# Squares of the residual taken early, the norm products placed later, rope tables inside the FFN, and the scores of two heads issued in turn into two banks

## The chip, the cores and the metric

The kernel runs on one core of one Trainium2 chip. The metric is the device time of one execution in microseconds, as the median of three runs. All times in this document are microseconds (us) unless marked ns. The engines are named as in the profile: PE is TensorE (PEld its weight loads), DVE is VectorE, ACT is ScalarE, POOL is GpSimd, SP is SyncE, which issues the DMAs.

## What is computed

Two networks of two layers each work one after the other on a residual stream x of 512 tokens by 1024 channels, in fp32 throughout. Each layer is a mixer followed by a gated FFN, and each of these eight parts has a norm before and a norm after:

```python
for l in range(2):                       # first block
    h = rms_norm(x, mix_norm_pre[l]) * (1.0 + sc_m) + sh_m
    y = hybrid_mixer(h, ...)             # 8-head attention over 256 selected keys, and a 4-head mLSTM
    x = x + g_m * rms_norm(y, mix_norm_post[l])
    h = rms_norm(x, ffn_norm_pre[l]) * (1.0 + sc_f) + sh_f
    y = swiglu(h, w_gate_up[l], w_down[l])
    x = x + g_f * rms_norm(y, ffn_norm_post[l])
# second block: the same frame, with another attention mixer, a convolution in the FFN, no modulation
```

The selection in the first block's attention takes, for each block of 128 queries, `relu(q_idx . k_idx)` of 8 index heads, weighted and summed, and keeps the top keys as a mask; the attention scores of each of the 8 heads (64 channels each) are then taken densely and masked.

## The kernel before, in words

All activations are kept transposed: 8 tiles (index k, `KT` = 8) of 128 channels by 512 tokens. Every large product is three fp32r products (`mm3`): high part of the weight with high part of the activation (`whi`, `hh`), `whi` with the low part `hl`, and `wlo` with `hh`. `load` (L261 to 267) brings a weight chunk by DMA into `raw`, copies it to `whi` on ACT and takes `wlo = raw - whi` on DVE.

**The passage from one part to the next.** The last projection of a part is computed in two halves of 256 tokens (`in_halves`): all output chunks for the first half, then the chunks in reverse order for the second half, the last few with weights that were kept. While PE computes the second half of the old projection, the first half goes through `post_norm` and `pre_norm`; while PE computes the first half of the next projection (`fm_split`), the second half goes through them. `post_norm` sums the squares of y with a product against a matrix of ones (tiles `nrm<-ssy`, `nrm<-sql`), takes the reciprocal root on ACT (`rstd`) and then on DVE does 8 times y * g * rstd (`yn`, L488) and x + yn (L489). `pre_norm` then squares the eight tiles of x on ACT (`sq<-x`, L444), adds them in pairs on DVE (L446), sums the four results over the channels with four products against ones (`nrm<-sq`), takes `rstd`, and writes `xn` (DVE L458), `hh` (ACT L462) and `hl` (DVE L473).

Where these products stand in PE's stream is set by numbers: `LA` = 2 and `LB` = 1 are the chunk of the old projection's second half before which the first half's `pre_norm` is called (after a mixer and after an FFN), `LC` = 4 and `LD` = 2 the chunk of the next projection's first half before which the second half's `pre_norm` (`pending`) is called. A scheduler then fixes one order per engine at build time; each engine runs its own list strictly in that order, waiting on semaphores. There are seven passages with a `pre_norm`: four from a mixer to its FFN (called M here), three from an FFN to the next mixer (called F).

**Rope tables.** At the start of the FFN of the first block's second layer, `rope_tables` computes cos and sin of the second block's positions: 128 x 512 operations on DVE and two Sin on ACT. In the FFNs `tick` advances a generator (`self.back`) by two steps after every chunk.

**Mixer of the first block.** Work is cut into generators whose steps a planner (`timeline`) merges by due times from a table (`T1`). `index(t)` makes the index scores of query block t (t = 1, 2, 3; 8 heads, (t + 1) * 128 keys); `topk(t)` turns them into a mask on DVE; `attend(hd)` makes for one head and t = 0 to 3 the scores (one plain fp32 product of 64 rows), adds mask and takes the row maximum on DVE (L872), and exponentiates on ACT; `attout(hd)` transposes the weights on PE and multiplies them with the values. Scores go into the two PSUM banks of the pool `pj`, which the projections of the same mixer use too. The two heads of a pair lie in rows 0 to 63 and 64 to 127 of the same tiles.

Of the kernel before, what the change touches and what calls it, by code (L numbers as in the profile page):

```python
# [10 lines left out]
F32 = mybir.dt.float32  # L11
# [3 lines left out]
ALU = mybir.AluOpType  # L15
# [23 lines left out]
PD1 = 0  # L39
PD2 = 0  # L40
EARLY = 6
PAIRS = 4
PH1 = 0
PH2 = 0
PXM = 0
SA = 0
LA = 2
LAG = 3
LOA = 40
NO = 7  # L50
LB = 1
LC = 4
LD = 2
WIN = 0
KF = 3
KM = 1
# [130 lines left out]
class Net:  # L187
# [174 lines left out]
    def norms(self, y, sqs, g, nxt, late):  # L362


        if nxt is None:
            steps = [lambda i=i: self.post_norm(HALVES[i], y, sqs, g, True) for i in range(2)]
            return {0: steps[0]}, steps[1], (None, None)
        h = self.new_h()
        post = [lambda i=i: self.post_norm(HALVES[i], y, sqs, g) for i in range(2)]
        pre = [lambda i=i: self.pre_norm(HALVES[i], *nxt, *h) for i in range(2)]  # L370
        self.pending = pre[1]
        if late == 0:
            return {0: lambda: (post[0](), pre[0]())}, post[1], h
        return {0: post[0], late: pre[0]}, post[1], h

    def fm_split(self, chunks, act, pool, more=None):

        tiles = [self.ps("pj" if i < PJ else "ps") for i, _ in enumerate(chunks)]  # L380

        begin = {LC if more is None else LD: self.pending}
        middle = {} if more is None else {0: lambda: run(steps(more, 4))}
        self.in_halves([(i, [src]) for i, src in enumerate(chunks)], KF if more is None else KM,
                       lambda i, ws, hs, _: self.fm(tiles[i], ws[0], 0, act, hs, range(KT)), pool,
                       begin, middle)
        return tiles
# [46 lines left out]
        run(self.tok_steps(*args))  # L434


    def pre_norm(self, hs, gs, sh, hh, hl):

        nc, x = self.nc, self.x
        ps = self.ps("nrm")  # L440
        sq = None
        for k in range(KT):
            s2 = self.half("sq")
            nc.scalar.activation(s2, x[k][:, hs], AF.Square)  # L444
            if sq is not None:
                nc.vector.tensor_tensor(s2, sq, s2, ALU.add)  # L446

            sq = s2 if k < 2 * PAIRS and k % 2 == 0 else None
            if sq is None:
                self.matmul(ps[:, :256], self.ones, s2, start=k == min(1, PAIRS), stop=k == KT - 1)  # L450
        r = self.half("rstd")
        self.ln_exp_rstd(ps[:, :256], r, D)
        ts = []
        for k in range(KT + LAG):
            if k < KT:
                t = self.half("xn")
                ts.append(t)
                nc.vector.scalar_tensor_tensor(t, x[k][:, hs], gs[:, k:k + 1], r, ALU.mult, ALU.mult)  # L458
                if sh is None:
                    nc.scalar.activation(hh[k][:, hs], t, AF.Copy)  # L460
                else:
                    nc.scalar.activation(hh[k][:, hs], t, AF.Identity, bias=sh[:, k:k + 1])  # L462
            if k >= LAG:
                j = k - LAG
                lo, hi = hl[j][:, hs], hh[j][:, hs].bitcast(F32)
                pool = (PH2 if sh is None else PH1) >> j & 1
                if sh is None:
                    (nc.gpsimd if pool else nc.vector).tensor_tensor(lo, ts[j], hi, ALU.subtract)
                elif pool:
                    nc.scalar.activation(ts[j], ts[j], AF.Identity, bias=sh[:, j:j + 1])  # L470
                    nc.gpsimd.tensor_tensor(lo, ts[j], hi, ALU.subtract)
                else:
                    nc.vector.scalar_tensor_tensor(lo, ts[j], sh[:, j:j + 1], hi, ALU.add, ALU.subtract)  # L473
# [68 lines left out]


    def rope_tables(self, pos):
        nc = self.nc
        cos = self.cp.tile([P, T], F32, tag="cos", name=self.nm("cos"))
        sin = self.cp.tile([P, T], F32, tag="sin", name=self.nm("sin"))
# [5 lines left out]
        for tab, turn in ((sin, 0.0), (cos, 0.25)):  # L553
            n = self.unit("n")
            nc.vector.tensor_scalar(n, ang, 1.0 / TWO_PI, turn, ALU.mult, ALU.add)
            nc.vector.tensor_scalar(n, n, MAGIC, None, ALU.add)
            nc.vector.tensor_scalar(n, n, MAGIC, None, ALU.subtract)
            r = self.unit("r")
            nc.vector.scalar_tensor_tensor(r, n, -C1, ang, ALU.mult, ALU.add)
            nc.vector.scalar_tensor_tensor(r, n, -C2, r, ALU.mult, ALU.add)  # L560
            nc.vector.scalar_tensor_tensor(r, n, -C3, r, ALU.mult, ALU.add)
            if turn:
                nc.vector.tensor_scalar(r, r, math.pi / 2, None, ALU.add)
            nc.vector.tensor_scalar(r, r, PI_IN, -PI_IN, ALU.min, ALU.max)
            self.act(tab, r, AF.Sin)
        self.cos, self.sin = cos, sin

    def rope(self, pa, pb, n=P):
# [39 lines left out]
    def scores(self, ps, q, k, n, qs):  # L608

        mm = self.matmul  # L610
        mm(ps[:, :n], q[:, qs], k[0][:, :n], start=True, stop=False)
        mm(ps[:, :n], q[:, qs], k[1][:, :n], start=False, stop=True)

    def softmax(self, ps, n, mask, gate=None):

# [63 lines left out]
    def mix1(self, l, h, nxt, feed=None):  # L679
# [126 lines left out]
        def index(t):  # L806
# [1 line left out]
            qs = slice(t * P, n)  # L808
            a = masks[t] = self.unit("ia")
            for hh in range(8):  # L810
                ps = self.ps("is")
                r = slice(64 * (hh % 2), 64 * (hh % 2) + 64)
                self.matmul(ps[:, :n], qi[hh // 2][r, qs], ki[r, :n], start=True, stop=True)
                w = cols[:, t, 4 + hh:5 + hh]
                if hh == 0:
                    nc.vector.tensor_scalar(a[:, :n], ps[:, :n], 0.0, w, ALU.max, ALU.mult)
# [43 lines left out]
            ka[g] = pairs(*self.rope(pa, pb))  # L860
            yield

        def attend(hd):
            g, i = divmod(hd, 4)
            r = slice(64 * (i % 2), 64 * (i % 2) + 64)
            probs[hd] = []
            for t in range(NB):
                n = (t + 1) * P
                ps, p = self.ps("pj"), self.unit("p")
                st = self.sp.tile([P, 1], F32, tag="st1", bufs=8, name=self.nm("st"))  # L870
                self.matmul(ps[:, :n], qa[g][i // 2][r, t * P:n], ka[g][i // 2][r, :n], start=True, stop=True)
                nc.vector.tensor_tensor_reduce(p[:, :n], ps[:, :n], self.tri if t == 0 else masks[t][:, :n], -0.125, 3.4e38,  # L872
                                               ALU.add, ALU.min, st)
                yield
                self.act(p[:, :n], p[:, :n], AF.Exp, bias=st, scale=-1.0)
                probs[hd].append(p)
                yield

        def attout(hd):
# [33 lines left out]
        s0, s1, ahead = w("at")  # L913
        d = (s1 - s0) / (8 + ahead)
        sc, at = [], []
        for hd in range(8):
            sc.append(Task(attend(hd), 8, s0 + d * hd, s0 + d * (hd + 1), {0: [pj[hd // 4]], 2: [tk[0]], 4: [tk[1]], 6: [tk[2]]}))
            at.append(Task(attout(hd), 13, s0 + d * (hd + ahead), s0 + d * (hd + ahead + 1), {0: [sc[hd], va_] + at[-1:]}))
        more = [Task(self.modulation(0, (2, 3, 4)), 24, *w("md"))] if l == 0 else []
        timeline(up_, va_, *cv, *ix, *tk, *pj, *ml, *sc, *at, *more)  # L920

# [174 lines left out]
    def block1(self, upto=None):  # L1096
# [20 lines left out]
        for l in range(2):  # L1117
# [11 lines left out]
                return t  # L1129

            if l == 1:
                self.rope_tables(A["positions_2"])
            gu, dn = A["w1_gu"][l], A["w1_dn"][l]
            h = self.ffn(h, lambda f, i: gu[2 * f + i], evict, lambda f, p: self.down_chunks(dn, f, p), self.modc(l, 5), nxt, (PF1, PD1))
            if upto == (1, l, "ffn"):
# [599 lines left out]
```

## Time and profile before

| | |
|---|---|
| median of 3 runs (lowest, highest) | 3197.48 us (3195.80, 3197.76) |
| profiled execution: own time, span | 3197.12 us, 3195.4 us |
| PE busy | 3044.9 us (95%) |
| PEld busy | 2545.4 us (80%) |
| DVE busy | 2013.8 us (63%) |
| ACT busy | 1548.1 us (48%) |
| POOL busy | 67.1 us (2%) |
| mean granted clock of TensorE | 0.978 |
| HBM read, written | 336.19 MB, 8.42 MB |

The span runs from the first to the last instruction of the profiled execution; the 1.7 us between it and that execution's own time lie around the instructions. Busy time of PE counts overlapping products once and includes the time that a product takes to drain, so that a busy PE is not one at its peak. Idle time of an engine counts for the end only where nothing else is on the way to it, so a wait is to be judged in its own stretch of the program. A granted clock of 1.00 is TensorE's upper level (2.4 GHz), 0.50 its lower (1.2 GHz).

### The profile page before, as it was taken

What the parts mean: (1) busy time and instruction counts of PE and PEld (TensorE: products, weight loads), DVE (VectorE), ACT (ScalarE), POOL (GpSimd) and SP (SyncE); (2) the same over time, 40 slices, a digit from 0 to 9 for tenths busy, and PEclk for the clock granted to TensorE, in tenths of its full rate; (3) what the DMA queues carried; (4) which work ended last, traced back from release to release, by engine and by line L of the source; (5) the groups of instructions that cost most, each with busy time, mean ns of one, the idle gap of its engine ahead of it and who ended that gap; (6) DMA issues with size and microseconds to landing.
All of it is one profiled execution on the core that took longest, in us unless ns stands there. A gap on an engine that the chain in (4) does not pass through costs nothing.

```text
span 3195.4 us, 42599 instructions
## 1 busy us (share of the span) xinstructions
PE 3044.9 (95%) x16196; PEld 2545.4 (80%) x16196; DVE 2013.8 (63%) x3692; ACT 1548.1 (48%) x2760; POOL 67.1 (2%) x179
## 2 busy tenths in 40 slices
PE   8998899998999899999999999999989999999998
PEld 6764788888875788888988779888888877898887
DVE  7887575546786563236676677635577766776365
ACT  4435542234445642234477665434445866454343
POOL 0000000000000000000000100000000001000000
PEclk9998999999999999999999999999999999999999
DMA  7244266644331232324421124333243112332323
GB/s 240 88 158 154 95 220 195 208 133 147 110 99 59 93 109 81 114 84 136 132 67 40 60 73 146 103 99 102 89 158 109 40 47 73 112 126 79 113 87 108
DMA packets 118925, 358.40 MB, mean 112 GB/s; under 512 B 15408, under 2 KB 28464, under 8 KB 118720
## 3 DMA queue, kind: packets, MB, share of 16 engines
q1 hardware_dynamic: 118720, 355.68, 34.2%
q8 instruction: 127, 2.08, 0.3%
q14 instruction: 78, 0.64, 0.1%
HBM read 336.19 MB, written 8.42 MB: 108 GB/s over the span
## 4 chain that ended last, share of the span: by engine, by line
PE 70%; issue 13%; DVE 10%; ACT 3%; DMA 3%; POOL 1%; SPq 0%; POOLq 0%; DVEq 0%; ACTq 0%
PE ps L305 28%; PE op L305 12%; PE pj L305 11%; PE dn L305 7%; PE tk L305 3%; PE po L305 2%; PE nrm L305 2%; DMA wm<-in_w_mod_dram 2%; DVE wlo L267 2%; DVE yn L488 1%; PE pt L308 1%; DVE x L489 1%; DVE wm L633 1%; DVE ss L1479 1%; PE cmp L305 1%
## 5 line engine op out<-in xcount | busy, mean ns | idle before, releaser
L267 DVE TENSOR_TENSOR wlo<-raw,whi 128x1024 fp32r<-128x1024 f32 (+1 forms) x562 | 628.7, 1123 | 577.8 <-ACT whi L265 575.4
L265 ACT ACTIVATE whi<-raw 128x1024 fp32r<-128x1024 f32 (+1 forms) x562 | 550.2, 980 | 803.3 <-PE ps L305 199.4
L305 PE MATMUL ps<-hh,whi 128*128 128x512 f32 (+1 forms) x1560 | 574.2, 368 | 0.0
L305 PE MATMUL ps<-hh,wlo 128*128 128x512 f32 (+1 forms) x1560 | 573.2, 367 | 0.0
L305 PE MATMUL ps<-hl,whi 128*128 128x512 f32 (+1 forms) x1560 | 572.5, 367 | 0.0
L305 PE MATMUL pj<-hh,whi 128*128 128x512 f32 (+1 forms) x944 | 352.8, 375 | 14.6 <-ACT hh L654 8.3
L305 PE MATMUL pj<-hl,whi 128*128 128x512 f32 (+1 forms) x944 | 351.5, 372 | 0.7 <-DVE hl L655 0.7
L305 PE MATMUL pj<-hh,wlo 128*128 128x512 f32 (+1 forms) x944 | 350.7, 371 | 0.1
L305 PEld LDWEIGHTS ps<-hh,wlo 128*128 128x128 f32 x1560 | 295.3, 189 | 48.8 <-DVE wlo L267 0.6
L305 PEld LDWEIGHTS ps<-hh,whi 128*128 128x128 f32 x1560 | 295.6, 189 | 48.1
L305 PEld LDWEIGHTS ps<-hl,whi 128*128 128x128 f32 x1560 | 295.3, 189 | 47.9
L305 PEld LDWEIGHTS pj<-hh,whi 128*128 128x128 f32 x944 | 179.5, 191 | 54.1 <-ACT hh L654 10.6
L305 PEld LDWEIGHTS pj<-hh,wlo 128*128 128x128 f32 x944 | 179.7, 190 | 30.3 <-issue 1.2
L305 PEld LDWEIGHTS pj<-hl,whi 128*128 128x128 f32 x944 | 179.8, 190 | 29.6 <-DVE hl L655 1.7
L633 DVE CUSTOM_DVE_ANT_0 wm<-wm,cact 128x1024 f32<-128x1024 f32 x96 | 116.9, 1221 | 108.4 <-DMA wm<-in_w_mod_dram 108.2
L305 PE MATMUL op<-hidh,whi 128*128 128x256 f32 (+1 forms) x572 | 178.5, 312 | 0.0
L305 PE MATMUL op<-hidh,wlo 128*128 128x256 f32 (+1 forms) x572 | 177.1, 310 | 0.3 <-DVE wlo L267 0.3
L305 PE MATMUL op<-hidl,whi 128*128 128x256 f32 (+1 forms) x572 | 176.5, 309 | 0.0
L305 PE MATMUL dn<-hidl,whi 128*128 128x512 f32 x352 | 137.0, 389 | 0.1
L305 PE MATMUL dn<-hidh,wlo 128*128 128x512 f32 x352 | 136.9, 389 | 0.0
L305 PE MATMUL dn<-hidh,whi 128*128 128x512 f32 x352 | 136.9, 389 | 0.0
L275 ACT ACTIVATE p<-p,st 128x128 f32<-128x128 f32 (+3 forms) x192 | 106.2, 556 | 57.7 <-DVE st L872 38.7
(350 smaller groups left out, 5804.0 us busy)
## 6 DMA issues: line engine op xcount, KB each, us to landing
raw<-in_w_in_dram SPq DMA_DIRECT2D x134, 512.0 KB, 3.4
raw<-in_w_up_dram SPq DMA_DIRECT2D x100, 512.0 KB, 3.5
wm<-in_w_mod_dram SPq DMA_DIRECT2D x96, 512.0 KB, 4.6
raw<-in_w_gu_dram SPq DMA_DIRECT2D x94, 512.0 KB, 3.5
raw<-in_w_dn_dram SPq DMA_DIRECT2D x80, 512.0 KB, 3.5
raw<-in_w_out_dram SPq DMA_DIRECT2D x52, 512.0 KB, 3.6
raw<-in_w_dn_dram SPq DMA_DIRECT2D x80, 192.0 KB, 3.1
hp<-rp SPq DMA_DIRECT2D x96, 64.0 KB, 2.0
```

The costliest lines, as they stand in the source:

```text
L265: nc_.scalar.activation(hi[:, :n], raw[:, :n], AF.Copy)
L267: (self.lo_eng or nc_.vector).tensor_tensor(lo[:, :n], raw[:, :n], hi[:, :n].bitcast(F32), ALU.subtract)
L275: j = self.nc.scalar.activation(out, in_, func, **kw).ins
L305: return self.paced(self.nc.tensor.matmul(*args, **kw))
L308: return self.paced(self.nc.tensor.transpose(*args))
L488: nc.vector.scalar_tensor_tensor(t, y(k, hs), g[:, k:k + 1], r, ALU.mult, ALU.mult)
L489: (nc.gpsimd if PXM >> k & 1 else nc.vector).tensor_tensor(self.x[k][:, hs], self.x[k][:, hs], t, ALU.add)
L633: self.nc.vector.tensor_tensor_reduce(raw, raw, self.cact, 1.0, 0.0, ALU.mult, ALU.add, self.mod[l][:, c:c + 1])
L1479: nc.vector.tensor_tensor_scan(s[:, c][:, ::-1], a[:, c][:, ::-1], a[:, c][:, ::-1], 0.0, ALU.add, ALU.bypass)
```

## The change

Four things, all in the order in which the same arithmetic is issued:

1. **Squares early, products late.** `pre_norm` loses its squares. A new `squares` (ACT squares, DVE pair sums) is called straight behind `post_norm` of the same half, and `pre_norm` begins with the four products. The first half's products are called two chunks later (`LA` 2 to 4, `LB` 1 to 3), the second half's one chunk later into an FFN (`LC` 4 to 5). Into a mixer they move from the first half of the projection (`LD`, dropped) to between the halves (`between`): one token step first where there are 3 chunks, none where there are 4, then the products, then the rest of four token steps. `PAIRS` (always pairs now) and the case `late == 0` go.
2. **Rope tables in steps.** `rope_steps` yields six times; the second layer's FFN takes it as its `self.back`, two steps per chunk.
3. **Index scores** of two heads are issued one behind the other (`two`), the second tied behind the first, into two banks, before the first is read.
4. **Attention scores**: `attend` takes a pair of heads instead of one; both products first, then both DVE operations, one step later both exponentials. Four tasks of 8 steps stand where there were eight of 8, over the same due times.

```diff
-LA = 2
+LA = 4
-LB = 1
-LC = 4
-LD = 2
+LB = 3
+LC = 5
...
         h = self.new_h()
-        post = [lambda i=i: self.post_norm(HALVES[i], y, sqs, g) for i in range(2)]
-        pre = [lambda i=i: self.pre_norm(HALVES[i], *nxt, *h) for i in range(2)]
-        self.pending = pre[1]
-        if late == 0:
-            return {0: lambda: (post[0](), pre[0]())}, post[1], h
-        return {0: post[0], late: pre[0]}, post[1], h
+        sq = {}
+
+        def post(i):
+            self.post_norm(HALVES[i], y, sqs, g)
+            sq[i] = self.squares(HALVES[i])
+
+        pre = lambda i: self.pre_norm(HALVES[i], sq[i], *nxt, *h)
+        self.pending = lambda: pre(1)
+        return {0: lambda: post(0), late: lambda: pre(0)}, lambda: post(1), h
...
-        begin = {LC if more is None else LD: self.pending}
-        middle = {} if more is None else {0: lambda: run(steps(more, 4))}
+        def between():
+            early = 4 - len(chunks)
+            run(steps(more, early))
+            self.pending()
+            run(steps(more, 4 - early))
+
+        begin, middle = ({LC: self.pending}, {}) if more is None else ({}, {0: between})
...
+    def squares(self, hs):
+
+        nc, x, res = self.nc, self.x, []
         for k in range(KT):
             s2 = self.half("sq")
             nc.scalar.activation(s2, x[k][:, hs], AF.Square)
-            if sq is not None:
-                nc.vector.tensor_tensor(s2, sq, s2, ALU.add)
-
-            sq = s2 if k < 2 * PAIRS and k % 2 == 0 else None
-            if sq is None:
-                self.matmul(ps[:, :256], self.ones, s2, start=k == min(1, PAIRS), stop=k == KT - 1)
+            if k % 2:
+                nc.vector.tensor_tensor(s2, res[-1], s2, ALU.add)
+                res.pop()
+            res.append(s2)
+        return res
+
+    def pre_norm(self, hs, sqs, gs, sh, hh, hl):
+
+        nc, x = self.nc, self.x
+        ps = self.ps("nrm")
+        for i, sq in enumerate(sqs):
+            self.matmul(ps[:, :256], self.ones, sq, start=i == 0, stop=i == len(sqs) - 1)
...
+    def two(self, tag, q, k, n, qs):
+
+
+        pss, last = [self.ps(tag) for _ in range(2)], None
+        for i, ps in enumerate(pss):
+            r = slice(64 * i, 64 * i + 64)
+            j = self.matmul(ps[:, :n], q[r, qs], k[r, :n], start=True, stop=True).ins
+            if last:
+                self.behind(j, last)
+            last = j.name
+        return pss
...
-                ps = self.ps("is")
-                r = slice(64 * (hh % 2), 64 * (hh % 2) + 64)
-                self.matmul(ps[:, :n], qi[hh // 2][r, qs], ki[r, :n], start=True, stop=True)
+                if hh % 2 == 0:
+                    pair = self.two("is", qi[hh // 2], ki, n, qs)
+                ps = pair[hh % 2]
...
-                ps, p = self.ps("pj"), self.unit("p")
-                st = self.sp.tile([P, 1], F32, tag="st1", bufs=8, name=self.nm("st"))
-                self.matmul(ps[:, :n], qa[g][i // 2][r, t * P:n], ka[g][i // 2][r, :n], start=True, stop=True)
-                nc.vector.tensor_tensor_reduce(p[:, :n], ps[:, :n], self.tri if t == 0 else masks[t][:, :n], -0.125, 3.4e38,
-                                               ALU.add, ALU.min, st)
-                yield
-                self.act(p[:, :n], p[:, :n], AF.Exp, bias=st, scale=-1.0)
-                probs[hd].append(p)
+                pss = self.two("pj", qa[g][i], ka[g][i], n, slice(t * P, n))
+                mask = self.tri if t == 0 else masks[t][:, :n]
+                ps_st = []
+                for ps in pss:
+                    p = self.unit("p")
+                    st = self.sp.tile([P, 1], F32, tag="st1", bufs=8, name=self.nm("st"))
+                    nc.vector.tensor_tensor_reduce(p[:, :n], ps[:, :n], mask, -0.125, 3.4e38, ALU.add, ALU.min, st)
+                    ps_st.append((p, st))
+                yield
+                for j, (p, st) in enumerate(ps_st):
+                    self.act(p[:, :n], p[:, :n], AF.Exp, bias=st, scale=-1.0)
+                    probs[2 * pr + j].append(p)
                 yield
...
             if l == 1:
-                self.rope_tables(A["positions_2"])
+                self.back = self.rope_steps(A["positions_2"])
```

How the change moves instructions is shown at three places.

**PE, first passage F** (first block, first layer, second half of the FFN's down projection: `op` are its chunks, 33 products each). Before, the four products on the squares stand 28 products behind the last product of the post norm (`nrm<-sql`):

```order
L305 MATMUL op_6539<-hidl_6090,whi_6468 128x256
L305 MATMUL op_6539<-hidh_6089,wlo_6469 128x256
L305 MATMUL nrm_6577<-sq_6580,ones 128x256
L305 MATMUL nrm_6577<-sq_6586,ones 128x256
L305 MATMUL nrm_6577<-sq_6592,ones 128x256
L305 MATMUL nrm_6577<-sq_6598,ones 128x256
L305 MATMUL op_6649<-hidh_5346,whi_6638 128x256
```

Now the first two stand 63 products behind it, two products into the third chunk (`op_6630`), and the other two 31 products further on:

```order
L303 MATMUL op_6580<-hidh_6060,wlo_6576 128x256
L303 MATMUL op_6630<-hidh_5317,whi_6619 128x256
L303 MATMUL op_6630<-hidl_5318,whi_6619 128x256
L303 MATMUL nrm_6668<-sq_6512,ones 128x256
L303 MATMUL nrm_6668<-sq_6517,ones 128x256
L303 MATMUL op_6630<-hidh_5317,wlo_6620 128x256
```

In the second half of F the first of these products stood 40 products behind `nrm<-sql` and stands 57 behind it now. In M, first half, 45 became 93; in M, second half, 24 products on the first half of the tokens lie behind them before the first product that reads the second half, where 48 lay before.

**ACT, the same passage.** Before, the eight squares stand behind the square of the next chunk's y (`sqy`), which waits for DVE:

```order
L275 ACTIVATE rstd_6512<-rstd_6512 128x256
L265 ACTIVATE whi_6688<-raw_6687 128x1024
L265 ACTIVATE whi_6694<-raw_6693 128x384
L1084 ACTIVATE sqy_6574<-y_3792 128x256
L444 ACTIVATE sq_6578<-x_3159 128x256
L444 ACTIVATE sq_6580<-x_3160 128x256
```

Now they stand ahead of it, and of two more weight splits:

```order
L263 ACTIVATE whi_6625<-raw_6624 128x384
L448 ACTIVATE sq_6510<-x_3130 128x256
L448 ACTIVATE sq_6512<-x_3131 128x256
L448 ACTIVATE sq_6515<-x_3132 128x256
L448 ACTIVATE sq_6517<-x_3133 128x256
L448 ACTIVATE sq_6520<-x_3134 128x256
L448 ACTIVATE sq_6522<-x_3135 128x256
L448 ACTIVATE sq_6525<-x_3136 128x256
L448 ACTIVATE sq_6527<-x_3137 128x256
L263 ACTIVATE whi_6709<-raw_6708 128x1024
L263 ACTIVATE whi_6715<-raw_6714 128x384
L1117 ACTIVATE sqy_6565<-y_3783 128x256
```

The square of y follows behind, and on DVE the first two pair sums now stand directly behind the sixteen operations of the post norm, with a weight split (`wlo`) between the second and the third sum.

**PE, attention scores** (first block, first layer; `pj<-hp,hp` are scores, both operands' tiles hold two heads). Before, neighbours are mostly of one head:

```order
L305 MATMUL pj_2254<-hp_1826,hp_1687 128x384
L305 MATMUL pj_2275<-hp_1827,hp_1688 128x128
L305 MATMUL pj_2293<-hp_1827,hp_1688 128x256
L305 MATMUL num_1994<-w_2247,vm_151 128x128
L305 MATMUL pj_2316<-hp_1827,hp_1688 128x384
L305 MATMUL pj_2353<-hp_1826,hp_1687 128x512
```

Now the two heads of a pair follow each other, but the scheduler has put another product between some:

```order
L303 MATMUL pj_2236<-hp_1833,hp_1696 128x384
L303 MATMUL pj_2237<-hp_1833,hp_1696 128x384
L303 MATMUL pj_2276<-hp_1834,hp_1697 128x128
L303 MATMUL pj_2277<-hp_1834,hp_1697 128x128
L303 MATMUL pj_2318<-hp_1834,hp_1697 128x256
L303 MATMUL num_2001<-w_2256,vm_151 128x128
L303 MATMUL pj_2319<-hp_1834,hp_1697 128x256
```

Of the 32 pairs of scores 22 are neighbours now, and 10 have one product between them; of the 24 pairs of index scores all are neighbours, where 20 were before.

## Rows read from the trace of the kernel before

**Rows 1.** The page, part 1: busy us, share of the span, instructions.
```profile
PE 3044.9 (95%) x16196; PEld 2545.4 (80%) x16196; DVE 2013.8 (63%) x3692; ACT 1548.1 (48%) x2760; POOL 67.1 (2%) x179
```
**Rows 2.** PE's waits by releaser: us in total, times, longest us.
```profile
PE nrm L305 <- DVE sq L446: 48.3, 11, 7.1
PE pj L305 <- DVE st L872: 11.8, 7, 7.7
```
**Rows 3.** Timeline, PE, four passages: start, us, what, [idle before, releaser].
```profile
375.45 0.80 PE L305 MATMUL nrm<-sq,ones 128*128 128x256 f32 x1 [3.74 <-DVE sq L446]
...
752.39 3.78 PE L305 MATMUL nrm<-sq,ones 128*128 128x256 f32 x8 [5.78 <-DVE sq L446]
...
782.75 1.13 PE L305 MATMUL nrm<-sq,ones 128*128 128x256 f32 x4 [2.54 <-DVE sq L446]
...
1141.81 3.86 PE L305 MATMUL nrm<-sq,ones 128*128 128x256 f32 x8 [7.13 <-DVE sq L446]
```
**Rows 4.** Windows, PE, five half-clock stretches at M: us, PE busy (x), PEclk, DMA.
```profile
374.60:381.40 6.80, 5.95 (x20) 0.50 0.45 155
...
sum 27.30, PE 21.92; mean PE 4.38
```
**Rows 5.** Windows, PE, the five half-clock stretches at F.
```profile
sum 30.80, PE 23.73; mean PE 4.75
```
**Rows 6.** Timeline, PE, behind the wait at 752 us: steps at both clocks.
```profile
756.40 0.41 PE L305 MATMUL op<-hidh,wlo 128*128 128x256 f32 x1
756.61 0.41 PE L305 MATMUL op<-hidh,whi 128*128 128x256 f32 x1
...
757.33 0.28 PE L305 MATMUL op<-hidh,wlo 128*128 128x256 f32 x1
757.45 0.28 PE L305 MATMUL op<-hidh,whi 128*128 128x256 f32 x1
```
**Rows 7.** Timeline, PE, the last product of the post norm there.
```profile
742.57 0.70 PE L305 MATMUL nrm<-sql,ones 128*128 128x256 f32 x2
```
**Rows 8.** Timeline, DVE, the same passage: post norm, split, pair sums.
```profile
744.26 0.88 DVE L488 SCALAR_TENSOR_TENSOR yn<-y,mod,rstd 128x256 f32<-128x256 f32 x2 [2.20 <-ACT rstd L275]
...
749.45 0.75 DVE L489 TENSOR_TENSOR x<-x,yn 128x256 f32<-128x256 f32 x2
...
750.45 1.22 DVE L267 TENSOR_TENSOR wlo<-raw,whi 128x1024 fp32r<-128x1024 f32 x1
...
751.92 0.75 DVE L446 TENSOR_TENSOR sq<-sq,sq 128x256 f32<-128x256 f32 x2
```
**Rows 9.** Timeline, ACT, the same passage: squares, rstd, first hh.
```profile
750.88 2.54 ACT L444 ACTIVATE sq<-x 128x256 f32<-128x256 f32 x8
756.21 0.48 ACT L275 ACTIVATE rstd<-nrm,eps 128x256 f32<-128x256 f32 x1 [2.78 <-PE nrm L305]
...
757.69 0.51 ACT L462 ACTIVATE hh<-xn,mod 128x256 fp32r<-128x256 f32 x1 [0.55 <-DVE xn L458]
```
**Rows 10.** Timeline, DVE, ahead of the wait at 1141 us: the rope tables begin.
```profile
1133.49 0.42 DVE L551 CAST ang<-pi 128x512 f32<-128x512 int32 x1
```
**Rows 11.** Windows, all engines: a passage F; the mixers of layers 0 and 1.
```profile
743.00:776.00 33.00, 26.23 (x189) 24.97 (x188) 26.48 (x55) 18.46 (x37) 0.00 (x0) 0.90 0.39 123
260.00:270.00 10.00, 1.92 (x6) 0.92 (x7) 10.00 (x23) 2.84 (x5) 0.00 (x0) 0.77 0.43 144
990.00:1050.00 60.00, 57.84 (x207) 30.48 (x206) 31.51 (x94) 42.30 (x86) 1.46 (x5) 0.95 0.14 44
```
**Rows 12.** Timeline, PE, index scores, one product (two records) and what follows.
```profile
135.12 1.12 PE L305 MATMUL is<-ki,hp 64*128 64x512 f32 x2
136.17 0.39 PE L305 MATMUL tk<-whi,hh 128*128 128x256 f32 x1
```
**Rows 13.** Timeline, PE, index scores of two heads (four records) and what follows.
```profile
139.24 1.13 PE L305 MATMUL is<-ki,hp 64*128 64x512 f32 x4
140.30 0.50 PE L305 MATMUL pj<-hh,whi 128*128 128x512 f32 x1
```
**Rows 14.** Timeline, DVE, the operation on a score of 512 keys.
```profile
268.95 0.67 DVE L872 CUSTOM_DVE_ANT_0 p<-pj,ia 128x512 f32<-128x512 f32 x1
```

More of the change, by code (lines that the diff above doesn't have):

```diff
@@ L41 @@
 EARLY = 6
-PAIRS = 4
 PH1 = 0
@@ L434, in tok @@
         run(self.tok_steps(*args))
[L437 to L441, printed above, removed]
+    def squares(self, hs):
+        nc, x, res = self.nc, self.x, []
         for k in range(KT):
@@ L544, in rope_tables, with rope_steps @@
     def rope_tables(self, pos):
+        run(self.rope_steps(pos))
+    def rope_steps(self, pos):
         nc = self.nc
@@ L561, in rope_tables @@
             nc.vector.scalar_tensor_tensor(r, n, -C3, r, ALU.mult, ALU.add)
+            yield
             if turn:
@@ L565, in rope_tables @@
             self.act(tab, r, AF.Sin)
+            yield
         self.cos, self.sin = cos, sin
@@ L861, in attproj, with attend @@
             yield
[L863 to L866, printed above, removed]
+        def attend(pr):
+            g, i = divmod(pr, 2)
+            probs[2 * pr], probs[2 * pr + 1] = [], []
             for t in range(NB):
                 n = (t + 1) * P
-                ps, p = self.ps("pj"), self.unit("p")
-                st = self.sp.tile([P, 1], F32, tag="st1", bufs=8, name=self.nm("st"))
-                self.matmul(ps[:, :n], qa[g][i // 2][r, t * P:n], ka[g][i // 2][r, :n], start=True, stop=True)
-                nc.vector.tensor_tensor_reduce(p[:, :n], ps[:, :n], self.tri if t == 0 else masks[t][:, :n], -0.125, 3.4e38,
-                                               ALU.add, ALU.min, st)
+                pss = self.two("pj", qa[g][i], ka[g][i], n, slice(t * P, n))
[6 more added lines that the diff above has]
+                    ps_st.append((p, st))
                 yield
-                self.act(p[:, :n], p[:, :n], AF.Exp, bias=st, scale=-1.0)
-                probs[hd].append(p)
+                for j, (p, st) in enumerate(ps_st):
+                    self.act(p[:, :n], p[:, :n], AF.Exp, bias=st, scale=-1.0)
+                    probs[2 * pr + j].append(p)
                 yield
@@ L915, in mix1 @@
         sc, at = [], []
+        for pr in range(4):
+            sc.append(Task(attend(pr), 8, s0 + d * 2 * pr, s0 + d * 2 * (pr + 1), {0: [pj[pr // 2]], 2: [tk[0]], 4: [tk[1]], 6: [tk[2]]}))
         for hd in range(8):
-            sc.append(Task(attend(hd), 8, s0 + d * hd, s0 + d * (hd + 1), {0: [pj[hd // 4]], 2: [tk[0]], 4: [tk[1]], 6: [tk[2]]}))
-            at.append(Task(attout(hd), 13, s0 + d * (hd + ahead), s0 + d * (hd + ahead + 1), {0: [sc[hd], va_] + at[-1:]}))
+            at.append(Task(attout(hd), 13, s0 + d * (hd + ahead), s0 + d * (hd + ahead + 1), {0: [sc[hd // 2], va_] + at[-1:]}))
         more = [Task(self.modulation(0, (2, 3, 4)), 24, *w("md"))] if l == 0 else []
```

## The prediction

> **What bounds the kernel now.** I read the page's busy line first, then PE's waits grouped by releaser, the timeline of PE at those waits, PE's granted clock behind them, and last DVE and ACT in the same stretches. PE is busy 3044.9 us of 3195.4, 95% [rows 1], and its list is strictly in order, so any time that PE loses is the kernel's. Little is idle, and it sits in few places. PE waits 11 times for a pair sum of squares, 48.3 us together [rows 2]: 3.74 us in the first half of each of the four passages M, 5.78 us in the first half of each of the three F, 2.54 us in the second half of the first F, and 7.13 us in one second half of M [rows 3]; 48.3 - 4 x 3.74 - 3 x 5.78 - 2.54 - 7.13 = 6.3 us are left for the second halves of the other two F.
>
> Each wait costs twice. Behind them stand ten stretches at a granted clock of 0.50, the lower level of 1.2 GHz; PE is busy in them 21.92 us at M and 23.73 us at F [rows 4, 5]. There a product follows the one before after 0.21 us, a moment later, at full clock, after 0.12 us [rows 6]. Of 45.65 busy us the share (0.21 - 0.12) / 0.21 = 0.43 is lost, 19.6 us. What can be had at the passages is 48.3 + 19.6 = **67.9 us**, of which M has 14.96 + 7.13 + 9.4 = 31.5 and F 17.34 + 8.84 + 10.2 = 36.4.
>
> **Squares early, products late: M.** In M's first half PE came to the first sum after 45 products of 0.12 us and waited 3.74 more, so the sum was ready 5.4 + 3.74 = 9.1 us behind `nrm<-sql`. Now 93 products, 11.2 us, lie there: nothing left. In the second half only 24 products, 2.9 us, lie behind the norm products before second-half columns of `hh` are read; from rstd's start to the end of the first `hh` it takes 757.69 + 0.51 - 756.21 = 2.0 us in F [rows 9], and DVE may be inside a split of 1.22 us when rstd ends [rows 8]. I leave 1 us in each M, 4 us in all.
>
> **F.** Its first half runs on DVE: `nrm<-sql` starts at 742.57 [rows 7], the sixteen post-norm operations begin at 744.26 and end at 749.45 + 0.75 = 750.2 [rows 8], and the eight squares follow on ACT in 2.54 us, the sums behind a split of 1.22 us [rows 8, 9]. With the squares ahead of the next splits on ACT, the first sum can be ready at about 750.6, 8.0 us behind `nrm<-sql`; 63 products cover 7.6 us, so 0.4 us of 5.78 are left. The split now stands between the second sum and the third (1.22 us), with 31 products (3.7 us) in between on PE, which cover it; but those products are of the chunk whose weights that split and its neighbours make, so I leave 1.5 us in all. In the second half 57 products cover 6.9 of the same 8.0 us: 1.5 us with the wait for the splits. Last comes the first use of h. DVE has 26.48 us of work in 33 us there [rows 11]; without the waits and the half clock the stretch shrinks by 5.78 + 0.43 x 4.75 = 7.8 us, to 25, where DVE has nothing to spare. I leave 2 us. Together 5 us in each F, 15 in all.
>
> The early squares cost ACT nothing that PE sees: they delay two weight splits by up to 2.54 us, and ACT is busy 18.46 us of those 33 [rows 11]; without that room it would be these 2.54 us in each half, 14 halves, 36 us. New waits keep some stretches at half clock: of 19.6 us I leave 5.
>
> **Rope tables.** 17 DVE operations of about 0.42 us, as the first [rows 10], are 7 us and stood ahead of the sums in the one M that waits 7.13 us [rows 3]. Two steps per chunk are about 2 us of DVE per chunk of an FFN; DVE is 63% busy over the whole [rows 1], and this hides. No DMA is added; the one that spreads the positions moves on SP's queue, among the weight loads of the same FFN. The price is bounded by nothing and by the 7 us.
>
> Norms and rope: 67.9 - 4 - 15 - 5 = **43.9 us**.
>
> **Scores.** An index score of 512 keys alone holds PE for 136.17 - 135.12 = 1.05 us [rows 12], two of different rows and banks for 140.30 - 139.24 = 1.06 us [rows 13]: neighbours run side by side. Only the 22 pairs that are neighbours gain; they hold 3328 columns in layer 0 and 3456 in layer 1 (of 5120 each), at 1.05 / 512 us 6.8 and 7.1 us of PE. Eight single index scores become four pairs: 4 x 1.05 = 4.2 us, half in each layer. In layer 0 little of it comes: up to about 290 us DVE is the bound (260 to 270: DVE 10.00 of 10, PE 1.92 [rows 11]), and I count only the last two pairs of heads, 1408 neighbouring columns, 2.9 us. In layer 1 PE is busy 57.84 of 60 us [rows 11]; there 7.1 + 2.1 count. Against this a pair needs both `pj` banks. PE waits for this bank only 11.8 us now [rows 2], and a bank comes free when DVE has read it, in 0.67 us [rows 14]; with a quarter of layer 1's 16 pairs waiting once, 2.6 us. Sum: 2.9 + 9.2 - 2.6 = **9.5 us**. The bounds are nothing and 6.8 + 7.1 + 4.2 = 18.1 us on the one side; below nothing, see the fourth rival.
>
> Rows 12 and 13 show only that PE gets through a pair in half the time. The Trainium skill, "TensorEngine Tiling (Array Packing)", section "PSUM Bottleneck", warns against counting on that: tiling speeds up TensorE but not the emptying of PSUM. By the rows the term is 9.5 us, by that rule taken strictly 0. The trace bears it out in layer 0, where DVE has no idle time, and not in layer 1, where it is busy 31.51 of 60 us [rows 11].
>
> **Sum.** The profiled execution took 3197.12 us, span and 1.7 us around it, 0.4 from the median 3197.48. 3197.1 - 43.9 - 9.5 = 3143.7: **3144 us**.
>
> **Rivals.**
> 1. *DVE becomes the bound of F.* For it: 26.48 busy us in a stretch that should shrink to 25. Against: the squares' sums are only 1.4 us of it, and PE had other products to do. F's 36.4 us all stay, M gives 31.5 - 4 - 1.5 = 26, the scores half: 3197.1 - 26 - 5 = 3166.
> 2. *The scores give nothing*, since the order of DVE's reads sets when banks come free, everywhere as in layer 0: 3153. For it the 260 to 270 window, against it layer 1 and that PE waits so little for `pj`. The Trainium skill, "TensorEngine Tiling (Array Packing)", section "PSUM Bottleneck", would lead here.
> 3. *Everything comes*: all waits and half-clock stretches go and all the PE time of the scores: 3197.1 - 67.9 - 18.1 = 3111. For it: 31 to 93 products of cover each; against: the sums of F above.
> 4. *Slower.* A pair's first score waits, and with it everything behind on PE (transposes, value products, mLSTM), until DVE has read both scores of the pair before; with DVE behind by several operations, in 32 pairs. It decides once a pair costs more than (43.9 + 6.4) / 32 = 1.6 us. At 2.5 us, four reads of 0.67 us: 3197.1 - 43.9 + 80 = 3233. Against it: 7 waits in all for this bank now, and DVE about half busy in layer 1 [rows 11].
> 5. *It does not do what it says.* The scheduler could move the products back; the order shows them later and the squares earlier, so only 10 of 32 pairs, split by another product, are left of this: no change, 3197.
>
> **How the numbers follow.** Forecast 0.55, rivals 0.15, 0.12, 0.12, 0.03, 0.03. The forecast's own range is 3125 (5 us in place of the 24 left at the passages) to 3158 (10 more left there, and 5 of the scores). The whole range takes in rivals 1 to 3 with a few us: 3110 to 3170. A measurement of this kernel can tell about 0.2%, 6.4 us, from no change; rivals 1 to 3 are faster by more. So faster 0.94, same 0.03, slower 0.03.
>
> **What would show it.** Right: PE's wait for a pair sum [rows 2] falls from 48.3 us to about 10; no half-clock stretch at M, at most short ones at F; behind the norm products small new waits for `wlo`, `hh` or `hl`; the record of a pair of `pj` scores as long as one; the 7.13 us wait gone with the rope operations spread over the FFN. Wrong: PE's waits at F move to `wlo` or `hl` with 5 us each (rival 1); PE's wait for `st` grows by what the pairs save (rival 2), or to tens of us (rival 4). The step I trust least is the 5 us in each F.

## The result and the profile after

The changed kernel takes 3151.65 us (median of 4 runs, 3147.71 to 3157.55) against 3196.64 of before: a ratio of 0.9861, 95% interval 0.9845 to 0.9876, 45 us less. In a second comparison, among the experiments below, it took 3152.74 against 3200.31, 0.985 (0.9837 to 0.9864). The forecast was 3144, in a range of 3110 to 3170: the time lies inside. But its two terms do not: the passages gave more than I forecast, and the paired scores cost time where I forecast a gain.

The page of the changed kernel, part 1, to be read beside [rows 1]: PE is busy 14.6 us less in a span that is 44.5 us shorter, so most of what went is waiting (a busy time counts products at half clock at their doubled length).

```profile
PE 3030.3 (96%) x16196; PEld 2532.9 (80%) x16196; DVE 2012.1 (64%) x3692; ACT 1545.4 (49%) x2758; POOL 66.7 (2%) x179
```

PE's waits by releaser, changed kernel (us in total, times, longest). The first line answers to the 48.3 us of [rows 2]. The next four are what took its place at the passages: the low part of h (`hl`), a weight split, and the high part of h. With the sums they make 8.0 us, of which one split of 0.3 us stood before, too. The wait for `st`, the score that DVE has not read yet, stands in total where it stood, 11.8 us [rows 2]; the wait of the value products for transposed weights (`pt`) grew from 7.9 us.

```profile
PE nrm L303 <- DVE sq L450: 1.7, 3, 0.7
...
PE pj L303 <- DVE hl L478: 3.1, 5, 0.9
...
PE pj L303 <- DVE hl L483: 1.6, 2, 0.9
...
PE op L303 <- DVE wlo L265: 1.4, 4, 0.3
...
PE tk L303 <- ACT hh L472: 0.2, 1, 0.2
...
PE pj L303 <- DVE st L903: 12.2, 7, 5.0
...
PE po L303 <- ACT pt L924: 12.7, 19, 1.7
```

Timeline of PE in the changed kernel (start, us, what, idle before and its releaser) in the first passage F and then in the second layer's M, to be read beside [rows 3, 7]. In F the first sums are used 750.40 - 742.31 = 8.09 us behind `nrm<-sql`, without a wait; a split is awaited for 0.34 us. In M the four products on the first half (two records each, at 1105.35) and the four on the second (at 1130.96, where 7.13 us were waited before) run without a wait.

```profile
742.31 0.70 PE L303 MATMUL nrm<-sql,ones 128*128 128x256 f32 x2
750.40 1.07 PE L303 MATMUL nrm<-sq,ones 128*128 128x256 f32 x4
751.81 0.39 PE L303 MATMUL op<-hidh,wlo 128*128 128x256 f32 x1 [0.34 <-DVE wlo L265]
755.62 1.02 PE L303 MATMUL nrm<-sq,ones 128*128 128x256 f32 x4
...
1105.35 1.89 PE L303 MATMUL nrm<-sq,ones 128*128 128x256 f32 x8
...
1120.58 0.59 PE L303 MATMUL nrm<-sql,ones 128*128 128x256 f32 x2
1130.96 1.89 PE L303 MATMUL nrm<-sq,ones 128*128 128x256 f32 x8
```

DVE in that F: the first two pair sums, directly behind the post norm (before: [rows 8]).

```profile
749.87 0.75 DVE L450 TENSOR_TENSOR sq<-sq,sq 128x256 f32<-128x256 f32 x2
```

Windows over the seven passages of the changed kernel, from 365, 735, 1093, 1463, 1922, 2291 and 2749 us and 50 to 60 us long (stretch, length, busy us of PE, PEld, DVE, ACT, POOL, then the granted clock, DMA share and GB/s): six of the seven stand at 1.00, where before ten stretches stood at 0.50 [rows 4, 5]. The one at 0.97 is shown with two others.

```profile
365.00:415.00 50.00, 49.90 (x394) 48.72 (x393) 41.85 (x89) 32.24 (x69) 0.00 (x0) 1.00 0.38 127
735.00:795.00 60.00, 57.13 (x444) 54.96 (x444) 48.42 (x103) 35.66 (x69) 0.82 (x4) 1.00 0.49 168
...
1463.00:1520.00 57.00, 54.47 (x414) 52.45 (x413) 46.80 (x101) 32.62 (x66) 2.08 (x4) 0.97 0.47 162
```

So by waits and clock the passages gave most of the 67.9 us, and yet only 44.5 are gone. A part was given back, most of it in the second layer's mixer. Between the first `nrm<-sql` of the first F and the last one of the second layer's M lie that passage F, the whole mixer and its output projection (operation and count, ns of one, first and last start). Before:

```profile
L305 PE MATMUL nrm<-sql,ones x8: 379/431/484, 742.6 to 1124.0; 128*128 128x256 f32 x8
```

and in the changed kernel:

```profile
L303 PE MATMUL nrm<-sql,ones x8: 378/379/483, 742.3 to 1120.8; 128*128 128x256 f32 x8
```

381.4 us became 378.5, although this stretch had 5.78 + 2.54 us of waits in F and 3.74 us in M's first half to lose [rows 3], and their half clock. The mixer got slower. The window over it, before and after, shows how: the granted clock fell.

```profile
930.00:1080.00 150.00, 134.67 (x538) 86.33 (x538) 98.79 (x212) 83.02 (x153) 4.80 (x14) 0.95 0.23 74
```

```profile
930.00:1080.00 150.00, 129.01 (x496) 79.92 (x495) 91.47 (x201) 78.58 (x145) 4.33 (x13) 0.90 0.22 66
```

And the timeline of PE there, in a stretch of 17.1 us at a clock of 0.50: one score product of 512 keys, two records, runs from 995.50 to 997.50, 2.0 us where [rows 12] has 1.05.

```profile
987.84 2.36 PE L303 MATMUL pj<-hp,hp 64*128 64x384 f32 x6 [1.17 <-DVE st L903]
990.69 1.43 PE L303 MATMUL pj<-hp,hp 64*128 64x128 f32 x4 [0.49 <-DVE st L903]
992.05 0.79 PE L303 MATMUL num<-w,vm 128*128 128x128 f32 x2
992.78 1.22 PE L303 MATMUL pj<-hp,hp 64*128 64x256 f32 x2
993.92 1.65 PE L303 MATMUL den<-ws,ones 128*128 128x384 f32 x2
995.50 2.07 PE L303 MATMUL pj<-hp,hp 64*128 64x512 f32 x2
997.50 2.08 PE L303 MATMUL nrm<-hr,ones 128*128 128x512 f32 x2
```

```profile
989.20:1006.30 17.10, 16.61 (x32) 6.44 (x31) 7.66 (x28) 8.48 (x17) 0.59 (x2) 0.50 0.00 1
```

At full clock two scores of a pair do run side by side: four records in 1.13 us, as long as one product, and then PE waits for `pt`.

```profile
1009.70 1.13 PE L303 MATMUL pj<-hp,hp 64*128 64x512 f32 x4
1011.66 1.12 PE L303 MATMUL po<-pt,va 128*128 128x512 f32 x2 [0.84 <-ACT pt L924]
```

### The profile page after: what moved, and what is told of

Its sections match the earlier page's. It is cut to its first block, busy times and chain, and to the rows that moved or that the text cites. A ratio compares the mean times of both kernels' runs of the same rounds, so it can differ in the third digit from the quotient of the medians.

```text
span 3150.9 us, 42591 instructions
## 1 busy us (share of the span) xinstructions
PE 3030.3 (96%) x16196; PEld 2532.9 (80%) x16196; DVE 2012.1 (64%) x3692; ACT 1545.4 (49%) x2758; POOL 66.7 (2%) x179
## 4 chain that ended last, share of the span: by engine, by line
PE 71%; issue 14%; DVE 9%; ACT 4%; DMA 1%; POOL 1%; SPq 0%; POOLq 0%; DVEq 0%; ACTq 0%
PE ps L303 29%; PE op L303 12%; PE pj L303 11%; PE dn L303 7%; PE tk L303 3%; PE po L303 3%; DVE wlo L265 2%; PE nrm L303 2%; PE pt L306 1%; DVE yn L498 1%; DMA wm<-in_w_mod_dram 1%; DVE ss L1512 1%; DVE x L499 1%; ACT whi L263 1%; PE cmp L303 1%
## 5 line engine op out<-in xcount | busy, mean ns | idle before, releaser
L303 PEld LDWEIGHTS ps<-hh,whi 128*128 128x128 f32 x1560 | 293.2, 189 | 48.3 <-ACT hh L472 0.4
L303 PE MATMUL tk<-whi,hh 128*128 128x256 f32 (+1 forms) x448 | 128.2, 288 | 0.2 <-ACT hh L472 0.2
```

The source lines that it names most:

```text
L303: return self.paced(self.nc.tensor.matmul(*args, **kw))
```

## The experiments

**The two halves of the change, each alone.** `e1_norms` keeps the scores of before, `e2_scores` the norms and rope tables of before; `e3_index` undoes the attention pairs alone.

The edit of `e1_norms` to the changed kernel, cut; `e3_index` has all of it but the first piece:

```diff
-                if hh % 2 == 0:
-                    pair = self.two("is", qi[hh // 2], ki, n, qs)
-                ps = pair[hh % 2]
+                ps = self.ps("is")
+                r = slice(64 * (hh % 2), 64 * (hh % 2) + 64)
+                self.matmul(ps[:, :n], qi[hh // 2][r, qs], ki[r, :n], start=True, stop=True)
...
-        def attend(pr):
...
+        def attend(hd):
...
-        for pr in range(4):
-            sc.append(Task(attend(pr), 8, s0 + d * 2 * pr, s0 + d * 2 * (pr + 1), {0: [pj[pr // 2]], 2: [tk[0]], 4: [tk[1]], 6: [tk[2]]}))
```

`e2_scores` is the kernel before with the opposite of these pieces and `two`.

> Only the early squares, later norm products and rope steps; the scores of before. Theory 1 (the passages gave about 61 us, the paired scores took some 16 back): 3197 - 61 = 3136, between 3130 and 3142, PE's waits for pair sums under 5 us, and the mixers of the first block within 3 us of before. Rival (the passages gave 35 to 44 as forecast, the scores 5 to 9, the rest of the shifts is chance): 3153 to 3162.

> Only the paired scores, index and attention; norms and rope tables of before. Theory 1: slower than before by 10 to 17 us, 3207 to 3214, with more time at a granted clock of 0.50 in the second layer's mixer. Rival (the scores gain as forecast): 3187 to 3192.

> The whole change but for the attention scores, which are issued by single heads as before; index scores in pairs. Theory 1, with the loss in the attention pairs alone: as e1_norms within 3 us, near 3136. Rival (the index pairs take part in the loss): 3 us or more above e1_norms.

Measured, against 3198.32 of before on the same chip: `e1_norms` 3142.59, ratio 0.9815 (0.9801 to 0.983), 55.7 us less; `e2_scores` 3209.06, 1.0032 (1.0022 to 1.0042), 10.7 us more; `e3_index` 3141.01, 0.9815 (0.9801 to 0.9828). The passages gave 55.7 us; the 61 expected were read from the shifts between two single profiles. The paired scores alone make the kernel slower. The index pairs show no effect, within 0.0014: the loss is in the attention pairs. Between the same two `nrm<-sql` as above, 381.4 us before, `e1_norms` takes 370.1:

```profile
L303 PE MATMUL nrm<-sql,ones x8: 379/379/483, 738.3 to 1108.4; 128*128 128x256 f32 x8
```

and `e2_scores` 394.8 (its profiled execution was the slowest of its twelve, 3217.89):

```profile
L305 PE MATMUL nrm<-sql,ones x8: 379/431/483, 747.6 to 1142.4; 128*128 128x256 f32 x8
```

with a granted clock of 0.86 in the mixer's window:

```profile
930.00:1080.00 150.00, 130.76 (x458) 79.00 (x457) 92.10 (x201) 74.05 (x132) 4.76 (x14) 0.86 0.24 70
```

**Is it the order, or what runs in it?** `e4_serial` and `e5_rows` keep the order and the banks of the change and alter the attention products alone: both heads in rows 0 to 63, so that none run side by side; or all 128 rows in each product. `e4_serial` leaves the second head's scores out, and `e5_rows` sums the two heads; PE's list of products is the same in both as in the change.

The edit of `e4_serial`:

```diff
-            r = slice(64 * i, 64 * i + 64)
+            r = slice(step * i, step * i + 64)
...
-                pss = self.two("pj", qa[g][i], ka[g][i], n, slice(t * P, n))
+                pss = self.two("pj", qa[g][i], ka[g][i], n, slice(t * P, n), 0)
```

and of `e5_rows`; `e6_after` is the changed kernel itself:

```diff
-            r = slice(64 * i, 64 * i + 64)
+            r = slice(64 * i, 64 * i + 64) if rows == 64 else slice(0, rows)
...
-                pss = self.two("pj", qa[g][i], ka[g][i], n, slice(t * P, n))
+                pss = self.two("pj", qa[g][i], ka[g][i], n, slice(t * P, n), P)
```

> The whole change, but both products of an attention pair take rows 0 to 63, so that they cannot run side by side; the order is that of the change, and the second head's scores are those of the first, which leaves the second head out. Theory 1 (the order and its waits set the time there, and PE's time saved by the pairs goes into waits): within 3 us of the change, 3149 to 3155. Rival (PE bounds layer 1, the time of products counts in full): up to 10 us above it, 3157 to 3162.

> The changed kernel, but each product of an attention pair contracts all 128 rows, so that the scores are sums over both heads; same order, same banks, and no two products side by side, as in e4_serial. Theory rows (the half clock in the second layer's mixer stays for 17 us because the products there use half of the rows): that stretch falls to 7 us or less as in e1_norms, and the time is 5 to 8 us under e4_serial, against before 0.985 or less. Theory order (the order and its waits set it): as e4_serial, ratio 0.986 to 0.989, the 17 us stretch stays.

> The changed kernel once more, on the same chip as the next three: 3148 to 3156, and 7 to 13 us above e1_norms.

Measured: `e4_serial` 3157.93 (against 3198.32), 0.9874 (0.9858 to 0.989); `e6_after` 3152.74 (against 3200.31), 0.985 (0.9837 to 0.9864); `e5_rows` 3134.62 on that same chip, 0.98 (0.9786 to 0.9813). Running side by side is worth little: `e4_serial` stands 0.0013 to 0.0024 above the two measurements of the change, 4 to 8 us, with intervals that overlap. That is nearer to the rival than to my 3 us, and it leaves the size open. `e5_rows` does settle its question. Its products do not run side by side, and it is 18.1 us faster than the change on the same chip; against `e4_serial`, by the ratios, it is 0.0074 or some 24 us faster, three times what I expected. The granted clock in the mixer's window, first `e4_serial`, then `e5_rows`:

```profile
930.00:1080.00 150.00, 131.54 (x481) 80.63 (x480) 90.87 (x199) 77.05 (x142) 3.99 (x12) 0.90 0.21 64
```

```profile
930.00:1080.00 150.00, 129.25 (x576) 89.25 (x575) 97.94 (x209) 83.96 (x156) 4.56 (x13) 0.97 0.27 79
```

With the same list on PE, twice the rows lift the clock from 0.90 to 0.97. One such window differs by some hundredths between two executions of one kernel: `e6_after`, the changed kernel again, has 0.86 there. But the sign that I had named holds in every profile: 64-row pairs have one half-clock stretch of 17.1 us between 985 and 1021 (the change, `e2_scores`, `e4_serial`, `e6_after`), `e5_rows` none longer than 6.8 us in that mixer.

What the clock costs shows when the whole mixer of the second layer is taken, from the last `nrm<-sql` of F to the first of M. In order the change, `e6_after`, `e4_serial`, `e5_rows` and, with single heads, `e1_norms`:

```profile
771.60:1093.70 322.10, 295.40 (x1488) 222.99 (x1487) 224.43 (x456) 163.65 (x285) 8.64 (x27) 0.94 0.29 93
768.20:1096.00 327.80, 300.42 (x1487) 225.35 (x1485) 224.53 (x456) 163.65 (x285) 8.76 (x27) 0.93 0.29 91
770.50:1094.90 324.40, 300.23 (x1488) 225.77 (x1486) 224.83 (x456) 163.87 (x285) 8.61 (x27) 0.94 0.29 92
770.30:1084.10 313.80, 287.30 (x1488) 223.47 (x1486) 224.61 (x456) 163.44 (x285) 8.92 (x27) 0.97 0.31 95
767.70:1081.30 313.60, 294.46 (x1488) 221.95 (x1487) 224.41 (x456) 163.57 (x285) 8.66 (x27) 0.97 0.30 96
```

Length times granted clock, an estimate of the mixer at full clock, is 303 to 305 us in all five (the rounding of the clock alone is 1.6 us): what sets them apart, 314 to 328 us, is the clock. What the pairs save on PE they give back in waits: PE is idle 26.7 us (322.10 - 295.40) in the change and 19.1 in `e1_norms`.

**What of the passages does it.** `n1_early` takes the squares early but leaves all products at their old places; `n2_late` has the new places, with the squares taken only there; `n3_norope` puts the rope tables back in one piece. All three are edits of `e1_norms`.

First `n1_early`:

```diff
-LA = 4
+LA = 2
...
-LB = 3
-LC = 5
+LB = 1
+LC = 4
+LD = 2
...
-        begin, middle = ({LC: self.pending}, {}) if more is None else ({}, {0: between})
+        begin = {LC if more is None else LD: self.pending}
+        middle = {} if more is None else {0: lambda: run(steps(more, 4))}
```

then `n2_late`:

```diff
-            sq[i] = self.squares(HALVES[i])
...
-        pre = lambda i: self.pre_norm(HALVES[i], sq[i], *nxt, *h)
+        pre = lambda i: self.pre_norm(HALVES[i], self.squares(HALVES[i]), *nxt, *h)
```

and `n3_norope`:

```diff
-                self.back = self.rope_steps(A["positions_2"])
+                self.rope_tables(A["positions_2"])
```

> e1_norms with the squares early but all products at their old places (LA 2, LB 1, LC 4, LD 2). Theory joint (at F the sums are ready about 8 us behind the post norm, and the cover there is 3.4 us again): about 4 us of wait per first half of F stay with their half clock, M's waits mostly go, the rope wait goes; 3160 to 3175. Rival (the early squares alone do it, the place does not matter): 3139 to 3146.

> e1_norms with all products at their new places, but the squares taken only there, behind the loads of that place. Theory joint: PE waits for the sums about as long as before at the new places, 3 to 6 us in each first half, the rope wait goes; 3170 to 3190. Rival (the place alone does it): 3139 to 3146.

> e1_norms with the rope tables in one piece ahead of the second layer's FFN, as before. Theory (the tables stood in the way of the sums of that one M): PE waits there for a pair sum or for hh 5 to 8 us again, with a half-clock stretch: 7 to 11 us above e1_norms, 3148 to 3156. Rival (with the squares early the tables do no harm): within 3 us of e1_norms.

Measured: `n1_early` 3187.88 (against 3200.31), 0.9955 (0.9942 to 0.9967); `n2_late` 3175.25, 0.9924 (0.9911 to 0.9938); `n3_norope` 3150.76 (against 3195.77), 0.9857 (0.9835 to 0.9879). With the rope steps in all of them, each half of the move alone gives 12 and 25 us, both together 55.7; a kernel with the rope steps alone was not run, and by `n3_norope` they are worth 0.0042 or some 13 us beside the two halves (8 us between the medians of two chips), so that little of the 12 need be the early squares. PE's wait for the sums says the same: 48.3 us before [rows 2], 33.6 in `n1_early`,

```profile
PE nrm L304 <- DVE sq L446: 33.6, 11, 4.0
```

25.9 in `n2_late`,

```profile
PE nrm L303 <- DVE sq L449: 25.9, 10, 3.0
```

and 1.9 in `e1_norms`:

```profile
PE nrm L303 <- DVE sq L450: 1.9, 3, 0.7
```

`n1_early` gave less than I expected: at M, too, the cover at the old places does not reach, and 3.07 us of wait are left at each M. With the tables in one piece the sums are in time, but what follows them on DVE is not: PE waits once, for `hh`, in `n3_norope`:

```profile
PE ps L303 <- ACT hh L472: 9.3, 1, 9.3
```

**A version that keeps 128 rows.** In `b1_padpairs` (on the change) and `b2_padsingle` (on `e1_norms`) each attention head has a tile of queries of its own, with zeros in the other head's 64 rows, and is multiplied with the keys of both heads; `b3_padall` is `b2_padsingle` with the index queries padded too. What is computed stays the same. The edit of `b2_padsingle` to `e1_norms`, cut; `b1_padpairs` hands the same padded tiles to `two`:

```diff
-        def pairs(o1, o2):
+        def pairs(o1, o2, pad=False):
...
-            ts = [self.unit("hp") for _ in range(2)]
+            ts = [self.unit("hp") for _ in range(4 if pad else 2)]
+            if pad:
+                for i, t in enumerate(ts):
+                    o = 64 - 64 * (i % 2)
+                    nc.gpsimd.memset(t[o:o + 64, :], 0.0)
...
-                    nc.sync.dma_start(ts[i // 2][r:r + 32, :], o[32 * i:32 * i + 32, :])
+                    nc.sync.dma_start(ts[i if pad else i // 2][r:r + 32, :], o[32 * i:32 * i + 32, :])
...
-                self.matmul(ps[:, :n], qa[g][i // 2][r, t * P:n], ka[g][i // 2][r, :n], start=True, stop=True)
+                self.matmul(ps[:, :n], qa[g][i][:, t * P:n], ka[g][i // 2][:, :n], start=True, stop=True)
```

> The changed kernel, computing everything, but with each attention head's queries in a tile of its own whose other 64 rows are zero (POOL writes the zeros), so that each score is a product of 128 rows; order and banks of the change. Theory rows, if rows of zeros count like others: as e5_rows, ratio 0.978 to 0.982, half clock in the second layer's mixer 10 us or less. Rival (the zeros do as little as the missing rows did): as the change or e4_serial, 0.985 to 0.989.

> e1_norms (scores by single heads as before) with the same zero-padded attention queries. Theory rows: 0.978 to 0.981, since e1_norms still has 17 us of half clock in the second layer's mixer and 34 in the first's, of which part goes. Rival: 0.981 to 0.983 as e1_norms.

> b2_padsingle with the index queries padded as well. Index scores lie where PE waits for little; the half clock near 130 us may go, but index products that now run side by side (20 pairs of 24) come one after the other and cost up to 1.05 us each more at 512 keys: within 5 us of b2_padsingle, rather above.

Measured, against 3195.77: `b1_padpairs` 3133.01, 0.9799 (0.9781 to 0.9818); `b2_padsingle` 3127.78, 0.978 (0.9761 to 0.9798); `b3_padall` 3120.88, 0.9762 (0.9744 to 0.9779). Rows of zeros count like others: the padded pairs are as fast as `e5_rows`. Padding helps the order of before as well, from 0.9815 in `e1_norms` to 0.978 (another chip; the intervals do not overlap), and single heads are no slower than pairs at 128 rows: 5.2 us faster, each of four runs below each of the pairs', though the intervals of the ratios overlap. I was wrong on the index queries: they gain rather than cost, 6.9 us, with all four runs (3119.83 to 3122.96) below all four of `b2_padsingle` (3123.09 to 3128.89), though here, too, the intervals overlap. In the mixer's window `e1_norms` has 0.94 (the other kernels with 64-row single heads have 0.94 to 0.97),

```profile
930.00:1080.00 150.00, 134.76 (x580) 88.16 (x579) 93.88 (x201) 82.62 (x155) 4.06 (x12) 0.94 0.25 78
```

`b2_padsingle` 1.00:

```profile
930.00:1080.00 150.00, 133.25 (x669) 96.75 (x668) 100.32 (x220) 87.21 (x173) 4.57 (x12) 1.00 0.25 80
```

`b3_padall` is the fastest kernel here: 74.9 us under before, and some 30 under the change.

## Why the prediction was right in its time and wrong in its parts

**M and F: the mechanism was right, the rest was sized too high.** The prize of 67.9 us and the reckoning of cover hold: the first sum of F was read 8.09 us behind `nrm<-sql` without a wait, and DVE had it some 8.0 us behind (about 0.4 us into the row of 749.87), where I had 8.0; M's first half waits for nothing, the 7.13 us wait is gone. The term that was mis-sized is what I left over, 4 us at M, 15 at F and 5 of half clock, 24 in all. By `e1_norms` it is 67.9 - 55.7 = 12.2, and the waits that the trace names at the passages make 8.0 us in the changed kernel. "I leave 2 us" for the first use of h and 1.5 for the splits were too much in each F: `hl` and `wlo` cost 3.1 + 1.6 + 1.4 us over all passages together. None of these waits is at an M, where I had left 4 us, and the one window at 0.97 is all that is left of the half clock, under 2 us where I had left 5. The rope term, 7.13 us and its half clock, shows in `n3_norope`, whose one wait is 9.3 us.

**Scores: wrong in sign.** I forecast a gain of 9.5 us; alone they cost 10.7 (1.0032), inside the change about as much (0.9861 and 0.985 against 0.9815 of `e1_norms`). The step that failed is "In layer 1 PE is busy 57.84 of 60 us [rows 11]; there 7.1 + 2.1 count". It took the price of a product, 1.05 us for 512 keys, as fixed, when [rows 11] showed that window at a mean clock of 0.95 and I did not ask what held it down. The price doubled for a while: in the 17.1 us at 0.50 a score of 512 keys took 2.0 us. That the rows bear on this is shown by `e5_rows` and `b1_padpairs`, with the same order and 128 rows. Why pairs of 64 rows fare worse than single heads of 64 rows (0.86 to 0.90 against 0.94 to 0.97 in the window) is not shown; that products of half the rows stand closer together there is a guess. The other term that was mis-sized is the 2.6 us of waits for the banks: PE's idle time in that mixer is 7.6 us larger than with single heads, and its length at full clock, 303 us against 304, shows no gain left.

**Rival 4 had the side, not the cause.** It let the pairs lose by waits for banks. PE's wait for `st` grew from 11.8 to 12.2 us only; in the second layer's mixer alone, between 950 and 1060, it is 3.1 us against 1.3 in `e1_norms`. The wait for `pt`, whose copies on ACT had the scores as cover, rose from 7.9 to 12.7 us and is 8.1 in `e4_serial`: it comes mostly with running side by side, not with the order.

```profile
PE po L303 <- ACT pt L924: 8.1, 13, 1.7
```

Rival 2 had a part: the time saved on PE went into waits. But the scores did not give nothing, they took, and that was the clock. The Trainium skill, "TensorEngine Tiling (Array Packing)", section "PSUM Bottleneck", warns that emptying PSUM does not speed up with tiling; the wait for `st` bears that out in the second layer with 1.8 us of the 7.6, and it is not what turned the gain into a loss. Rival 3 did not come.

**The sum.** -55.7 and about +10.7 make -45.0, as measured; I had -43.9 and -9.5. That the time lay in the range is luck: 12 us of caution at the passages stood against 20 us of error in the scores. A right total is no evidence for its terms.

## What to carry to other kernels

Where an engine in strict order waits for a chain on others, begin the chain earlier and also read its result later: each alone gave 12 and 25 us here, both gave 56 (rope steps, worth up to 13 us, included each time). Before counting on TensorE time saved by small products side by side, look at the granted clock of that window and ask what the products do to it. Contracting zeros beside 64 useful rows costs a single product no time on PE, and here it bought back most of the upper clock.

## What the runs showed of the hardware

The number of rows in a product bears on the clock that the throttle grants: with the same list on PE the mixer's window went from 0.86 to 0.90 (the change twice and `e4_serial`, 64 rows) to 0.97 (`e5_rows`, 128), and from 0.94 to 1.00 by padding with zeros (`e1_norms`, `b2_padsingle`). Against a single product of 64 rows the cost in PE time is nothing (what is given up is the second product that could run beside it [rows 13]): a score of 512 keys by 128 rows, in `b2_padsingle`, starts at 980.85 and the next product at 981.81, 0.96 us, against 1.05 for 64 rows [rows 12].

```profile
980.85 1.13 PE L303 MATMUL pj<-hp,hp 128*128 128x512 f32 x2 [1.28 <-DVE st L903]
981.81 1.02 PE L303 MATMUL nrm<-hr,ones 128*128 128x512 f32 x2
```

The zeros are written by POOL, in 0.52 us for 64 rows of 512, as the groups of `b3_padall` show:

```profile
L812 POOL MEMSET hp<- 64x512 f32 x32 | 16.7, 521 | 149.8 <-DVE yn L498 114.4 <-DVE mod L678 18.1 <-PE nrm L303 9.9
```

Whether these kernels spread more from one execution to the next because of where the clock falls was not tried. The spreads on record do not settle it: the changed kernel's four runs lie 9.8 us apart at first and 2.8 in `e6_after`, those of the kernel before 2.4 to 12.1, those of `b3_padall` 3.1.
